# One encoder layer on one core: a weight sum on GpSimd, a copy on ScalarE, swapped chunk pools, longer planned waits and an earlier store

## The chip, the core and the metric

The kernel runs on one core of a Trainium2 chip. The metric is the device time of one execution in microseconds (us). The engines are named as in the profile: PE is TensorE (matmuls; PEld its weight loads), DVE is VectorE, ACT is ScalarE, POOL is GpSimd, SP is SyncE, which issues most DMAs. L90 is line 90 of the kernel.

## The reference

One layer on x of 512 tokens by 1024 channels, all in float32. RMSNorm, then one projection whose columns feed three branches and their sigmoid gates; an output projection with a residual; RMSNorm, SwiGLU with 2816 hidden columns, a residual and a last RMSNorm.

```python
h = rms_norm(x, norm1_g)
u_pool, aq, ak, av, rq, rf, rb, ri, rg, gate_pre = split_cols(h @ w_in)
y_pool = pool_mixer(u_pool, pool_w, pool_scale)
y_attn = diff_attention(aq, ak, av, lam, diff_norm_g, lambda_init)   # 4 heads, two key/query parts each
y_rec = hgrn2_mixer(rq, rf, rb, ri, rg, lb_fwd, lb_bwd, hgrn_norm_g) # 4 heads, scans in both directions
gates = sigmoid(gate_pre)
merged = sum(gates[i] * (y[i] @ w_up[i]) for i in range(3))
x = x + merged @ w_out
gu = rms_norm(x, norm2_g) @ w_ffn_in
x = x + (silu(gu[:, :2816]) * gu[:, 2816:]) @ w_ffn_out
return rms_norm(x, final_norm_g)
```

## The kernel before

**Precision.** Most products are made of three matmuls. Each operand is split into a high part (`whi`, `hT_hi`: a cast on ACT) and a low part (`wlo`, `hT_lo`: the value less its high part, a subtraction on DVE), and hi·hi, hi·lo and lo·hi are summed in PSUM. A weight thus costs a load by SP into a ring of two buffers (`wraw`), a cast on ACT (L185) and a subtraction on DVE (L186) into a ring of three (`wsp`). `Jobs.pump` writes these ahead of the jobs that need them: at most two chunks of the ring that still have unsplit parts, at most three parts held (four in the feed-forward stage). A chunk with a `where` is loaded into a pool of its own as soon as that pool exists and isn't counted among the two. All weight loads are chained in one order on SP.

**Order.** TensorE's instructions keep the order in which the program writes them (`keep_in_program_order` in `mm`, L89, and `transpose`, L97). That order is made by a small planner, `Pipe` (L40 to L74): streams of work (the heads of a mixer and the stream of projection jobs) yield either `("w", us)`, wait so long in planned time, or `("e", event, us)`, wait until so long after an event. The first stream in the list that is free goes next. Planned time is counted from matmul sizes alone; a stall on the chip is unknown to it. The other engines' orders are chosen by a scheduler that simulates the program when it is built; `tc.issue_after(i)`, also through `behind`, keeps what it encloses behind instruction `i` on `i`'s own engine, and does nothing to instructions of another engine.

**PSUM.** `bank("mm")` and `bank("rc")` have three buffers each, `bank("tp")` two.

The places that the change touches, in order of time:

- *Start* (L566 to L597): `norm1_g` is transposed on PE and spread over the partitions in two halves, each copied from PSUM into `g_b` by DVE (L577). `norm_rows` takes a square sum on ACT (L477), rstd on POOL (L148, L142), then multiplies the row by rstd and `g_b` on DVE in two halves (L483). `rows_T` transposes them on PE (L98) into `hT`.
- *Recurrence* (`rec_scan`, L869): after its scan a head waits for the event "V" (the values) and a planned 1.0 us, makes six states (`st`) of `kT` and `v_rec` in two "rc" banks, waits a planned 1.6 us, and makes its outputs in another "rc" bank.
- *Attention* (`att_head`, L1034): a head's first scores wait until 6.0 us after its query and key projections (event `AF{h}`). Scores are two matmuls for each of two parts, with `k` and with `l`, its rest, of which one half is copied by ACT (L1025).
- *First output quarter* (L1253): `quarter_parts` makes two chunks of 256 columns of `w_out`. The first goes to the pool "wx" (made at L1748, when the gate stage's pools have been closed), the second to the ring.
- *Feed-forward*. The 22 column pairs go through a two by two scheme (Strassen-like, seven products for eight) on sums of activation blocks, the "forms" (`Forms.make`: DVE L356, ACT L359), and on sums of weight blocks, which `PairChunk.add` (L259) makes with three DVE additions: 1024 wide (L263) and twice 512 wide (L266, L267) into one buffer, `sums`. A pair has four jobs, `first` to `fourth`; `PairPart.sums_and_split` casts the sums (`shi`, L302) and subtracts (`slo`, L304). Pair 2's sums are written in `third` of pair 1 (L1343), behind the forms' last instructions. `g` (L1350) and `u` (L1355) add PSUM into SBUF, and pair 2's splits stand behind pair 1's `g` on DVE.
- *Tail* (`seven_job`, L1602): four row blocks of the output get their last products, the residual add (L1410), squares (ACT, L1417), the final gain (DVE, L1419), rstd (POOL, L142) and the two halves of `out_store`: ACT scales one and issues its store, DVE the other, SP its store.

Of the kernel before, what the change touches and what calls it, by code (L numbers as in the profile page):

```python
# [33 lines left out]
def strided(t, offset, dims):  # L34

    return bass.AP(tensor=t.tensor, offset=t.offset + offset, ap=[list(t.ap[0])] + [list(d) for d in dims])
# [40 lines left out]
def encoder_kernel(ctx: ExitStack, tc: tile.TileContext, x, norm1_g, w_in, pool_w, pool_scale,  # L77
# [111 lines left out]
    class Jobs:  # L189
# [10 lines left out]
        def add(self, parts, body):  # L200
            self.jobs.append((parts, body))
            for p in parts:
                if p not in self.parts:
                    self.parts.append(p)
                if p.chunk not in self.chunks:
                    self.chunks.append(p.chunk)
# [37 lines left out]
    class PairChunk:  # L244
# [11 lines left out]
                last = nc.sync.dma_start(out=self.raw[:, c], in_=src).ins  # L256
            return last

        def add(self):  # L259
            half = KT // 2 * P  # L260
            sums = self.sums = LAST["ws"].tile([P, 4, half], F32, name="sums", bufs=1)
            w11, w12 = strided(self.raw, 0, [[1, half]]), strided(self.raw, half, [[1, half]])
            nc.vector.tensor_tensor(out=strided(sums, 0, [[2 * half, 2], [1, half]]),  # L263
                                    in0=strided(self.raw, 0, [[3 * half, 2], [1, half]]),
                                    in1=strided(self.raw, 2 * half, [[0, 2], [1, half]]), op=ALU.add)
            nc.vector.tensor_tensor(out=sums[:, 3], in0=sums[:, 2], in1=w11, op=ALU.add)  # L266
            nc.vector.tensor_tensor(out=sums[:, 1], in0=sums[:, 3], in1=w12, op=ALU.add)  # L267

    @contextmanager
    def behind(after):  # L270
# [170 lines left out]
    def quarter_parts(w, c0, n, where=None, skip=0):  # L441

        v = w.rearrange("(kt p) c -> p kt c", p=P)
        for c in range(0, n, 256):
            ch = Chunk(v[:, :, c0 + c:c0 + c + 256], KT, 256, where if c == 0 else None)
            yield slice(c, c + 256), [Part(ch, lambda raw, j=j: raw[:, j:j + 4, :], 4, 256, None, skip)
                                       for j in (0, 4)]

# [124 lines left out]
    for half in range(2):  # L573
        gt = bank("rc", (P, 4, P))
        for j in range(4):
            transpose(gt[:, j, :], g_cols[:, half * 4 + j:half * 4 + j + 1].to_broadcast([P, P]), ident)
        nc.vector.tensor_copy(out=g_b[:, half * 512:half * 512 + 512], in_=gt.rearrange("p a b -> p (a b)"))  # L577

    probe = xg.tile([P, 1024], F32R, name="probe")
    nc.scalar.copy(out=probe, in_=ident.rearrange("p (o c) -> p o c", o=1).to_broadcast([P, 8, P]))  # L580
# [288 lines left out]
    def rec_scan(h):  # L869
# [64 lines left out]
            nc.scalar.copy(out=kT[:, 3 * d:3 * d + 3, :], in_=ps[:, 0:3, :])  # L934
        mark(f"S{h}")
        yield ("e", "V", 0.8)
        yield ("w", 1.0)
        st = rh.tile([P, 6, P], F32, name="st", bufs=2)
        vs = [v_rec[:, b, h * P:(h + 1) * P] for b in range(NB)]
        for d in range(2):  # L940
# [4 lines left out]
            for prev, j in zip((None,) + order, order):  # L945
                own = st[:, 3 * d + j, :]
                if prev is None:
# [2 lines left out]
                total = strided(pyr, toff + d * S + j + d, [[1, 1]])  # L950
                nc.vector.scalar_tensor_tensor(out=own, in0=st[:, 3 * d + prev, :], scalar=total, in1=ps[:, j, :],
                                               op0=ALU.mult, op1=ALU.add)
        yield ("w", 1.6)
        ps = bank("rc")
        for b in range(NB):
            o = ps[:, b * P:(b + 1) * P]
# [77 lines left out]
    def att_head(h):  # L1034
        if h:
            yield ("e", f"QK{h - 1}", 0.0)
        if h > 1:
            yield ("e", f"AN{h - 2}", 0.0)
        yield ("e", f"AF{h}", 6.0)
        t = att.pop(h)  # L1040
        at, (vh, vl), aT, y_attn = ATT["at"], ATT["v"], ATT["aT"], ATT["y"]
        strip = ATT["strip"].tile([P, 896], F32, name="strip")
        nc.sync.dma_start(out=strip, in_=c_dist[h])
        zz = at.tile([P, NB, 2], F32, name="zz")
        rr = at.tile([P, NB], F32, name="rr")
        probs = {}

        def scores(i):
            bs = slice(i * P, (i + 1) * P)
            mx = small.tile([P, 2], F32, name="mx")  # L1050
            ex = []
            for c in range(2):
                ps = bank("rc")
                mm(ps, t[f"q{c}"][:, bs], t[f"k{c}"], True, False)
                mm(ps, t[f"q{c}"][:, bs], t[f"l{c}"], False, True)
                s = at.tile([P, S], F32, name=f"s{c}")

                nc.vector.tensor_tensor_reduce(out=s, in0=strip[:, 384 - P * i:896 - P * i], in1=ps, scale=1.0,  # L1058
                                               scalar=3.0e38, op0=ALU.add, op1=ALU.min, accum_out=mx[:, c:c + 1])
                nc.scalar.activation(out=s, in_=s, func=AF.Exp, scale=-1.0, bias=mx[:, c:c + 1],  # L1060
                                     accum_out=zz[:, i, c:c + 1])
                ex.append(s)

            co = small.tile([P, 2], F32, name="co")
            zn, co = co[:, 0:1], co[:, 1:2]
            nc.gpsimd.tensor_tensor(out=zn, in0=zz[:, i, 0:1], in1=nlam, op=ALU.mult)
            nc.gpsimd.tensor_tensor(out=co, in0=zz[:, i, 1:2], in1=minus1, op=ALU.pow)
            nc.gpsimd.tensor_tensor(out=co, in0=co, in1=zn, op=ALU.mult)
            nc.vector.scalar_tensor_tensor(out=ex[0], in0=ex[1], scalar=co, in1=ex[0], op0=ALU.mult, op1=ALU.add)
            probs[i] = ex[0]  # L1070

        def turn(i):
            bs = slice(i * P, (i + 1) * P)
            p = probs.pop(i)
            pt = bank("tp", (P, NB, P))
            for k in range(NB):
                transpose(pt[:, k, :], p[:, k * P:(k + 1) * P], ident)
            nc.scalar.copy(out=aT[0][:, :, bs], in_=pt)
            nc.vector.tensor_tensor(out=aT[1][:, :, bs], in0=pt, in1=aT[0][:, :, bs].bitcast(F32), op=ALU.subtract)

        scores(0)
        for i in range(NB):
            yield ("w", 1.6 + (0.7 if i == 0 else 0.0))
            if i + 1 < NB:
                scores(i + 1)
            else:
                mark(f"QK{h}")
            yield ("w", 2.4 + (1.0 if i + h == 0 else 0.0))
            if h and i == 0:
                yield ("e", f"PV{h - 1}", 0.0)  # L1090
            turn(i)
        mark(f"T{h}")
        nc.vector.reciprocal(out=rr, in_=zz[:, :, 0])
        yield ("e", "VA", 1.5)
        yield ("w", 1.5)
        ps = bank("rc")
        es = slice(h * P, (h + 1) * P)
        terms = [(vh, aT[0]), (vl, aT[0]), (vh, aT[1])]
        for i, (a, r) in enumerate(terms):
            for k in range(NB):  # L1100
                mm(ps, a[:, k, es], r[:, k, :], i == 0 and k == 0, i == 2 and k == NB - 1)
            yield
        mark(f"PV{h}")
        og, rbp = yield from head_norm(ps, at, gain_a, rr, 1)
        mark(f"AN{h}")
        nc.vector.tensor_tensor(out=og, in0=og, in1=rbp, op=ALU.mult)
        nc.scalar.copy(out=y_attn[0][:, h, :], in_=og)
        nc.vector.tensor_tensor(out=y_attn[1][:, h, :], in0=og, in1=y_attn[0][:, h, :].bitcast(F32),
                                op=ALU.subtract)
# [202 lines left out]
    def ffn_pair_bodies(j):  # L1312
# [30 lines left out]
        def third(part):  # L1343
            f = FF["forms"]
            if j == 1:
                with behind(FF["forms_end"]):
                    pairs[2][1].chunk.add()
            c["sl"] = FF["t"].tile([P, S], F32, name="silu")
            yield from product(c["x"], part, 0, f.d, False)
            on_dve = nc.vector.tensor_tensor(out=c["g"], in0=c["x"], in1=c["g"], op=ALU.add).ins  # L1350
            if j == 1:
                FF["g1"] = (on_dve,)
            nc.scalar.activation(out=c["sl"][:, 256:], in_=c["g"], func=AF.Silu, scale=-1.0)
            yield from product(c["y"], part, 1, f.r22, False)
            nc.vector.tensor_tensor(out=c["u"], in0=c["u"], in1=c["zy"], op=ALU.add)  # L1355
# [56 lines left out]
    def out_sums(b, c0, w, col, out_=None):  # L1412

        x = out_cols(b, c0, w)
        junk = FF["t"].tile([P, S], F32, name="silu")
        col = 4 * b + col
        sq = nc.scalar.activation(out=junk[:, 0:w], in_=x, func=AF.Square, scale=D ** -0.5,  # L1417
                                  accum_out=FF["stats"][:, col:col + 1]).ins
        nc.vector.tensor_tensor(out=x if out_ is None else out_, in0=x, in1=FF["g"][:, c0:c0 + w], op=ALU.mult)  # L1419
        return sq  # L1420
# [181 lines left out]
    def seven_job():  # L1602
# [81 lines left out]
        sv_product(x[1][:, first], 7, 1, False, True, first)  # L1684
        out_add(3, 256, x[1][:, second], ALU.subtract)
        out_add(3, 0, x[1][:, first], ALU.subtract)
        out_sums(3, 0, 256, 1, src[:, first])
        sv_product(own[:, second], 7, 1, True, True, second)
        out_add(3, 256, own[:, second], ALU.subtract)
        sq = out_sums(3, 256, 256, 2, src[:, second])  # L1690
        rstd, on_dve = out_rstd(3, 3)
        with behind((sq, on_dve)):
            out_store(2, late)
        out_store(3, rstd, src)
        yield

    for i, (j, _) in enumerate(PLAIN):
# [137 lines left out]
```

## Time and profile before

| | us |
|---|---|
| median of three runs | 881.21 |
| lowest, highest | 880.99, 881.6 |
| profiled execution, its time | 880.92 |
| its span, first to last instruction | 879.0 |
| PE busy | 866.3 |
| DVE, ACT, POOL busy | 660.8, 448.9, 37.8 |

A timeline row reads: start, time taken, engine, line, operation, output<-input, shape, number of instructions merged into the row, and in brackets the idle time before it with what ended it. A merged row's time runs from its first start to its last end. The profile's waits and busy times are of one execution.

### The profile page before, as it was taken

Reading aid. Unit: us, or ns where it says so; the run is one execution under the profiler, and the core shown is the slowest. Engines: PE = TensorE matmul, PEld = TensorE weight load, DVE = VectorE, ACT = ScalarE, POOL = GpSimd, SP = SyncE. Lnnn points to the kernel's source line nnn. Section 1 sums busy time; section 2 is a strip of 40 time slices with the busy share of each in tenths; the row PEclk is TensorE's granted clock in tenths of the full one; section 3 lists DMA queues with packets and bytes.
Section 4 is the critical chain, followed back from the end, with each engine's and each line's share of the span. In section 5 each row is a group of like instructions: output and inputs, shape, how many; then the busy total and the mean of one; then the engine's idle time right before and its main releaser. Section 6 shows DMA issues by size and latency. Waiting matters only on the chain.

```text
span 879.0 us, 14111 instructions
## 1 busy us (share of the span) xinstructions
PE 866.3 (99%) x5713; PEld 786.4 (89%) x5713; DVE 660.8 (75%) x978; ACT 448.9 (51%) x718; POOL 37.8 (4%) x83
## 2 busy tenths in 40 slices
PE   8999999999999999999999999999999999999996
PEld 7989988888997888899999898999999999988885
DVE  6788655854757787987876645997888888847996
ACT  6544333525747764563355335755655655533563
POOL 2000000000112230000000001000000000000001
PEclk9999999999999999999999999999999999999999
DMA  8330113124133131343331770253433433355002
GB/s 244 97 120 25 50 48 96 48 73 138 45 96 94 52 104 48 97 134 107 96 97 48 263 192 1 54 139 106 135 97 98 137 102 98 120 192 191 1 1 97
DMA packets 115694, 87.54 MB, mean 100 GB/s; under 512 B 3862, under 2 KB 104748, under 8 KB 115628
## 3 DMA queue, kind: packets, MB, share of 16 engines
q1 hardware_dynamic: 115036, 85.57, 32.2%
q8 instruction: 45, 0.74, 0.4%
q10 hardware_dynamic: 592, 1.05, 0.3%
q14 instruction: 21, 0.17, 0.1%
HBM read 84.52 MB, written 2.10 MB: 99 GB/s over the span
## 4 chain that ended last, share of the span: by engine, by line
PE 86%; issue 7%; DVE 3%; DMA 2%; ACT 1%; POOL 1%; POOLq 0%; DVEq 0%; ACTq 0%
PE mm L90 56%; PE rc L90 26%; PE tp L90 2%; PE tp L98 2%; DMA raw<-in_w_out_dram 1%; DVE wlo L186 1%; DVE hrow L483 1%; DMA raw<-in_w_in_dram 0%; ACT whi L185 0%; DVE hT_lo L500 0%; PE rc L98 0%; ACT s L1060 0%; POOL rso L142 0%; DVE g1b L577 0%; ACT l L1025 0%
## 5 line engine op out<-in xcount | busy, mean ns | idle before, releaser
L185 ACT CAST whi<-raw 128x1024 fp32r<-128x1024 f32 (+1 forms) x134 | 127.6, 958 | 141.5 <-PE mm L90 90.7
L186 DVE TENSOR_TENSOR wlo<-raw,whi 128x1024 fp32r<-128x1024 f32 (+1 forms) x134 | 147.5, 1106 | 51.2 <-ACT whi L185 35.4
L90 PE MATMUL mm<-hT_hi,whi 128*128 128x512 f32 (+1 forms) x344 | 82.4, 371 | 0.0
L90 PE MATMUL mm<-hT_hi,wlo 128*128 128x512 f32 (+1 forms) x344 | 81.4, 370 | 0.2 <-DVE wlo L186 0.2
L90 PE MATMUL mm<-hT_lo,whi 128*128 128x512 f32 (+1 forms) x344 | 81.1, 369 | 0.0
L304 DVE TENSOR_TENSOR slo<-sums,shi 128x1024 fp32r<-128x1024 f32 x58 | 70.6, 1218 | 0.3 <-ACT shi L302 0.3
L90 PEld LDWEIGHTS mm<-hT_hi,whi 128*128 128x128 f32 x344 | 59.0, 189 | 9.8 <-ACT hT_hi L496 0.4
L90 PEld LDWEIGHTS mm<-hT_lo,whi 128*128 128x128 f32 x344 | 59.1, 189 | 9.5
L90 PEld LDWEIGHTS mm<-hT_hi,wlo 128*128 128x128 f32 x344 | 58.7, 189 | 9.6 <-DVE wlo L186 0.4
L302 ACT CAST shi<-sums 128x1024 fp32r<-128x1024 f32 x58 | 61.0, 1052 | 4.6 <-DVE sums L266 3.7
L263 DVE TENSOR_TENSOR sums<-raw 128x1024 f32<-128x1024 f32 x29 | 35.4, 1219 | 1.5 <-DMA raw<-in_w_in_dram 1.5
L90 PE MATMUL mm<-y_arena,whi 128*128 128x512 f32 x128 | 32.5, 394 | 0.0
L90 PE MATMUL mm<-whi,y_arena 128*128 128x256 f32 (+1 forms) x192 | 31.9, 316 | 0.2 <-ACT whi L185 0.2
L916 DVE TENSOR_TENSOR kq<-kq,pyr 128x256 f32<-128x256 f32 x48 | 18.2, 421 | 18.1 <-PE rc L90 18.0
L90 PE MATMUL rc<-kq,kc 128*128 128x128 f32 x224 | 31.6, 285 | 0.0
L90 PEld LDWEIGHTS rc<-kq,kc 128*128 128x128 f32 x224 | 30.1, 191 | 1.5
L90 PEld LDWEIGHTS mm<-whi,y_arena 128*128 128x128 f32 x192 | 27.4, 188 | 3.2 <-ACT whi L185 0.8
L885 ACT COPY kc<-kq 128x512 f32<-128x512 f32 x28 | 18.6, 666 | 20.4 <-PE rc L90 12.7
L1060 ACT ACTIVATE s<-s,mx 128x512 f32<-128x512 f32 x32 | 23.1, 721 | 10.9 <-DVE mx L1058 10.7
L90 PEld LDWEIGHTS mm<-y_arena,whi 128*128 128x128 f32 x128 | 23.8, 188 | 5.0
L1350 DVE TENSOR_TENSOR g<-mm,g 128x256 f32<-128x256 f32 x21 | 8.9, 424 | 23.7 <-PE mm L90 23.7
L90 PE MATMUL mm<-fhi,slo 128*128 128x256 f32 x168 | 26.1, 278 | 0.6 <-DVE slo L304 0.5
(386 smaller groups left out, 2045.7 us busy)
## 6 DMA issues: line engine op xcount, KB each, us to landing
raw<-in_w_in_dram SPq DMA_DIRECT2D x44, 512.0 KB, 4.1
raw<-in_w_ffn_in_dram SPq DMA_DIRECT2D x44, 512.0 KB, 5.3
raw<-in_w_in_dram SPq DMA_DIRECT2D x8, 1024.0 KB, 5.2
raw<-in_w_ffn_out_dram SPq DMA_DIRECT2D x7, 1024.0 KB, 4.9
raw<-in_w_out_dram SPq DMA_DIRECT2D x4, 1024.0 KB, 11.1
xin<-in_x_dram SPq DMA_DIRECT2D x4, 512.0 KB, 4.6
raw<-in_w_up_rec_dram SPq DMA_DIRECT2D x2, 1024.0 KB, 6.6
raw<-in_w_up_pool_dram SPq DMA_DIRECT2D x2, 1024.0 KB, 5.1
```

Of the source, the lines that this page charges most:

```text
L90: i = nc.tensor.matmul(out_, lhsT=lhsT, rhs=rhs, start=start, stop=stop, skip_group_check=chain)
L98: tc.keep_in_program_order(nc.tensor.transpose(out_, in_, idn))
L185: nc.scalar.copy(out=hi, in_=view)
L186: LAST["wlo"] = nc.vector.tensor_tensor(out=lo, in0=view, in1=hi.bitcast(F32), op=ALU.subtract).ins
L263: nc.vector.tensor_tensor(out=strided(sums, 0, [[2 * half, 2], [1, half]]), in0=strided(self.raw, 0, [[3 * half, 2], [1, half]]), in1=stri ...
L302: nc.scalar.copy(out=hi, in_=view)
L304: on_dve = nc.vector.tensor_tensor(out=lo, in0=view, in1=hi.bitcast(F32), op=ALU.subtract).ins
L483: on_dve = nc.vector.scalar_tensor_tensor(out=h[:, cs], in0=src[:, cs], scalar=rstd, in1=g_b[:, cs], op0=ALU.mult, op1=ALU.mult).ins
L885: nc.scalar.copy(out=strided(kc, 0, [[2 * n, S // (2 * n)], [n, 2], [1, n]]), in_=strided(kq, 2 * S, [[2 * n, S // (2 * n)], [S + n, 2], [ ...
L916: nc.vector.tensor_tensor(out=xv, in0=xv, in1=tv, op=ALU.mult)
L1060: nc.scalar.activation(out=s, in_=s, func=AF.Exp, scale=-1.0, bias=mx[:, c:c + 1], accum_out=zz[:, i, c:c + 1])
L1350: on_dve = nc.vector.tensor_tensor(out=c["g"], in0=c["x"], in1=c["g"], op=ALU.add).ins
```

## The change

Seven edits:

1. `PairChunk.add` takes an engine, and pair 2's three additions go to POOL. The other pairs' stay on DVE.
2. In `quarter_parts` the second chunk of the first output quarter goes to "wx" and the first to the ring.
3. The second half of `g_b` is copied by ACT.
4. In the recurrence, head 1 waits a planned 4.5 us instead of 1.0 after the values.
5. Heads 0 and 1 wait a planned 2.4 us instead of 1.6 before their outputs.
6. In the attention, heads 2 and 3 wait 7.0 us instead of 6.0 after their projections.
7. Block 2's scaling and store are written after the first half of block 3's sums instead of after its rstd; they stand behind that half's square on ACT, where before they stood behind the second half's square on ACT and rstd's addition on DVE.

```diff
-        def add(self):
+        def add(self, eng=None):
+            eng = eng or nc.vector
...
-            nc.vector.tensor_tensor(out=strided(sums, 0, [[2 * half, 2], [1, half]]),
+            eng.tensor_tensor(out=strided(sums, 0, [[2 * half, 2], [1, half]]),
...
-            nc.vector.tensor_tensor(out=sums[:, 3], in0=sums[:, 2], in1=w11, op=ALU.add)
-            nc.vector.tensor_tensor(out=sums[:, 1], in0=sums[:, 3], in1=w12, op=ALU.add)
+            eng.tensor_tensor(out=sums[:, 3], in0=sums[:, 2], in1=w11, op=ALU.add)
+            eng.tensor_tensor(out=sums[:, 1], in0=sums[:, 3], in1=w12, op=ALU.add)
...
-            ch = Chunk(v[:, :, c0 + c:c0 + c + 256], KT, 256, where if c == 0 else None)
+            ch = Chunk(v[:, :, c0 + c:c0 + c + 256], KT, 256, where if c else None)
...
-        nc.vector.tensor_copy(out=g_b[:, half * 512:half * 512 + 512], in_=gt.rearrange("p a b -> p (a b)"))
+        (nc.scalar.copy if half else nc.vector.tensor_copy)(
+            out=g_b[:, half * 512:half * 512 + 512], in_=gt.rearrange("p a b -> p (a b)"))
...
-        yield ("w", 1.0)
+        yield ("w", 4.5 if h == 1 else 1.0)
...
-        yield ("w", 1.6)
+        yield ("w", 2.4 if h < 2 else 1.6)
...
-        yield ("e", f"AF{h}", 6.0)
+        yield ("e", f"AF{h}", 7.0 if h > 1 else 6.0)
...
                 with behind(FF["forms_end"]):
-                    pairs[2][1].chunk.add()
+                    pairs[2][1].chunk.add(nc.gpsimd)
...
-        out_sums(3, 0, 256, 1, src[:, first])
+        with behind((out_sums(3, 0, 256, 1, src[:, first]),)):
+            out_store(2, late)
...
-        sq = out_sums(3, 256, 256, 2, src[:, second])
-        rstd, on_dve = out_rstd(3, 3)
-        with behind((sq, on_dve)):
-            out_store(2, late)
-        out_store(3, rstd, src)
+        out_sums(3, 256, 256, 2, src[:, second])
+        out_store(3, out_rstd(3, 3)[0], src)
```

More of the change, by code (lines that the diff above doesn't have):

```diff
@@ L262, in add @@
             w11, w12 = strided(self.raw, 0, [[1, half]]), strided(self.raw, half, [[1, half]])
-            nc.vector.tensor_tensor(out=strided(sums, 0, [[2 * half, 2], [1, half]]),
-                                    in0=strided(self.raw, 0, [[3 * half, 2], [1, half]]),
-                                    in1=strided(self.raw, 2 * half, [[0, 2], [1, half]]), op=ALU.add)
-            nc.vector.tensor_tensor(out=sums[:, 3], in0=sums[:, 2], in1=w11, op=ALU.add)
-            nc.vector.tensor_tensor(out=sums[:, 1], in0=sums[:, 3], in1=w12, op=ALU.add)
+            eng.tensor_tensor(out=strided(sums, 0, [[2 * half, 2], [1, half]]),
+                              in0=strided(self.raw, 0, [[3 * half, 2], [1, half]]),
+                              in1=strided(self.raw, 2 * half, [[0, 2], [1, half]]), op=ALU.add)
+            eng.tensor_tensor(out=sums[:, 3], in0=sums[:, 2], in1=w11, op=ALU.add)
+            eng.tensor_tensor(out=sums[:, 1], in0=sums[:, 3], in1=w12, op=ALU.add)
     @contextmanager
```

## The prediction

> **What bounds the kernel now.** I read the page's first part, then what the TensorE (PE) row waits for, then the timeline around each of its gaps.
>
> ```profile
> span 879.0 us, 14111 instructions
> PE 866.3 (99%) x5713; PEld 786.4 (89%) x5713; DVE 660.8 (75%) x978; ACT 448.9 (51%) x718; POOL 37.8 (4%) x83
> ```
>
> TensorE is the bound: 99% of the span, its order written out by a planner. An edit beside it gains only what it takes out of a PE gap, plus what it takes from the stretch behind the last matmul. The profiled execution took 880.92 us, 1.9 more than its span; the three plain runs have a median of 881.21. Sums are made against 880.92; I add 0.29 at the end. Differences under 0.2% (1.8 us) can't be told from none here.
>
> A gap is measured from start to start, since a matmul's end is modelled past the point where the next one can issue: four 128x256 matmuls issue in 0.45, though their row says 0.62 or 0.73. The diff touches six gaps, in order of time.
>
> **Start.** The second half of the gain vector is copied out of PSUM by VectorE (DVE) between the first and second half of the first norm row.
>
> ```profile
> 7.51 1.05 ACT L185 CAST whi<-raw 128x1024 fp32r<-128x1024 f32 x1 [0.57 <-DMA raw<-in_w_in_dram]
> 7.51 0.68 DVE L577 COPY g1b<-rc 128x512 f32<-128x512 f32 x1
> ...
> 8.23 2.08 DVE L483 SCALAR_TENSOR_TENSOR hrow<-xin,rstd,g1b 128x512 f32<-128x512 f32 x3
> ...
> 9.04 0.65 PE L98 MATMUL tp<-ident,hrow 128*128 128x128 f32 x4 [0.73 <-DVE hrow L483]
> ...
> 15.08 2.35 DVE L186 TENSOR_TENSOR wlo<-raw,whi 128x1024 fp32r<-128x1024 f32 x2
> ...
> 16.43 1.05 POOL L148 TENSOR_SCALAR ms<-ss 128x1 f32<-128x1 f32 x1 [2.77 <-ACT hrow L477]
> ...
> 20.22 1.25 PE L98 MATMUL tp<-ident,hrow 128*128 128x128 f32 x8 [0.18 <-DVE hT_lo L500]
> ...
> 39.08 0.58 ACT L895 COPY pt<-rc 128x512 f32<-128x512 f32 x1
> ```
>
> On ScalarE (ACT) the copy costs 0.58 (last row, same shape out of PSUM) and fits the 0.57 in which ACT waits for a weight, from 6.94 (7.51 - 0.57) on. The second half row then starts at 7.6 instead of 8.23: 0.63 for the transposes at 9.04 and all behind them. It must also survive 20.22, where PE waits for work behind the fourth block's norm. That norm's GpSimd (POOL) step at 16.43 took 1.05 because it ended with the DVE pair of 15.08 (17.43), and that pair moves up too. I take 0.55. If the third weight load binds instead, 0; if the simulated schedule puts the copy ahead of ACT's second square, again 0.
>
> **Recurrence.** Heads 0 and 1 make their states back to back.
>
> ```profile
> 115.17 1.50 PE L90 MATMUL rc<-v_rec,kT 128*128 128x128 f32 x12
> ...
> 117.19 0.91 PE L90 MATMUL rc<-v_rec,kT 128*128 128x128 f32 x6 [0.51 <-DVE pt L924]
> ...
> 118.53 0.91 PE L90 MATMUL rc<-v_rec,kT 128*128 128x128 f32 x6 [0.44 <-ACT st L948]
> ...
> 119.19 0.70 PE L90 MATMUL mm<-hT_hi,whi 128*128 128x512 f32 x2
> ```
>
> At 0.11 apiece (118.53 to 119.19 for six), twelve take 1.32 and six 0.66: lost 2.02 - 1.32 = 0.70 and 1.34 - 0.66 = 0.68, together 1.38, waiting for "rc" banks to be emptied. The longer planned wait puts head 1 some 3.5 us later, and projection matmuls that wait for nothing stand in between. The work is the same, only its order changes. The new order has three banks too: a scan level, head 0's output and head 1's two states want four, so one shorter wait may come back. I take 1.2, between 0.6 and 1.38.
>
> **Attention.** Head 2's first scores wait for its second key part.
>
> ```profile
> 277.74 0.40 PE L90 MATMUL rc<-l,q 128*128 128x512 f32 x1
> ...
> 278.51 0.62 ACT L1025 CAST l<-l 64x512 fp32r<-64x512 f32 x1
> ...
> 279.18 0.50 PE L90 MATMUL rc<-l,q 128*128 128x512 f32 x1 [0.81 <-ACT l L1025]
> ...
> 279.52 1.09 PE L90 MATMUL mm<-hT_hi,whi 128*128 128x512 f32 x4
> ```
>
> The wait makes the first matmul after it cost 0.11 more (a row of four 0.73 instead of 0.62), so a 512-wide one takes 0.34 - 0.11 = 0.23 (279.18 to 279.52). From 277.74 stand two, 0.46, and 1.44 passed: 0.98, and 0.11 for the restart, 1.09 lost. One microsecond later the key part (279.13) is there. The planner runs the head's next scores behind the previous head's value product anyway, so the stage's end doesn't move. I take 1.0; if head 3's tail does come later, 0.4 is left.
>
> **First output quarter.** Its first weight chunk sits in a pool whose space comes free only when the gate forms have been read.
>
> ```profile
> 486.51 6.51 SPq L164 DMA_DIRECT2D raw<-in_w_out_dram  x3
> ...
> 496.20 2.00 ACT L185 CAST whi<-raw 128x1024 fp32r<-128x1024 f32 x2 [2.15 <-DMA raw<-in_w_out_dram]
> ...
> 497.30 0.73 PE L90 MATMUL mm<-whi,y_arena 128*128 128x256 f32 x4
> ...
> 500.63 1.54 PE L90 MATMUL mm<-whi,y_arena 128*128 128x256 f32 x12
> ```
>
> Eighteen matmuls stand between the two PE rows, 2.04 at 0.113; 3.33 passed, 1.29 lost. With the pools swapped the first chunk loads into the ordinary ring, ahead of 486.51, and its splits lie before 497. The second chunk takes the late space, issued at about 486.5, there by 496, and is not wanted before 506. SP's queue behind it (the next chunk, the norm gain) moves up or stays. I take 1.2 (0.9 to 1.29).
>
> **Tail.** Block 2's stores move from behind block 3's last sums to between its two halves.
>
> ```profile
> 870.91 0.42 ACT L1417 ACTIVATE silu<-x 128x256 f32<-128x256 f32 x1 [1.55 <-DVE x L1410]
> ...
> 873.12 0.71 ACT L1441 ACTIVATE x<-x,rstd 128x512 f32<-128x512 f32 x1
> ...
> 875.06 0.34 ACTq L1442 DMA_DIRECT2D out_dram<-x  x1
> ```
>
> The same by windows (PE, PEld, DVE, ACT, POOL busy, then clock, DMA share, GB/s), and the page's row of these stores:
>
> ```profile
> 874.00:875.00 1.00, 0.00 (x0) 0.00 (x0) 0.49 (x1) 0.69 (x1) 0.28 (x1) 1.00 0.23 90
> 875.00:876.00 1.00, 0.00 (x0) 0.00 (x0) 0.00 (x0) 0.03 (x1) 0.00 (x0) 1.00 1.01 387
> ...
> out_dram<-x ACTq DMA_DIRECT2D x4, 256.0 KB, 2.6
> ```
>
> The last four stores (1.05 MB) go out together at 387 GB/s, 2.7 us from about 874.8. With block 2's scaling at 871.4 its half is gone by then, and block 3's 0.52 MB takes 1.35 from about 875.8: some 0.5 less. Next late is block 3's own chain (sums, rstd, scaling), not shortened. The added work on ACT (0.71 and an issue) fits before the second square; the other issue goes to SP, which has nothing else queued. I take 0.5 (0.2 to 0.9).
>
> These five sum to 0.55 + 1.2 + 1.0 + 1.2 + 0.5 = 4.45 (ends 2.1 and 5.2).
>
> **The sums on GpSimd.**
>
> ```profile
> 560.90 1.22 DVE L304 TENSOR_TENSOR slo<-sums,shi 128x1024 fp32r<-128x1024 f32 x1
> ...
> 562.04 0.69 DVE L186 TENSOR_TENSOR wlo<-raw,whi 128x512 fp32r<-128x512 f32 x1
> 562.64 1.22 DVE L356 TENSOR_TENSOR flo<-hid,fhi 128x1024 fp32r<-128x1024 f32 x1
> ...
> 563.78 1.22 DVE L263 TENSOR_TENSOR sums<-raw 128x1024 f32<-128x1024 f32 x1
> ...
> 564.74 0.62 PE L90 MATMUL rc<-h_hi,slo 128*128 128x256 f32 x4
> ...
> 564.92 0.42 DVE L1350 TENSOR_TENSOR g<-mm,g 128x256 f32<-128x256 f32 x1
> ...
> 575.11 0.62 PE L90 MATMUL rc<-h_hi,shi 128*128 128x256 f32 x4
> ```
>
> Two POOL rows of the attention, the DVE row beside the first, and the two POOL groups from which a rate can be had:
>
> ```profile
> 238.94 0.55 POOL L1067 TENSOR_TENSOR co<-zz,fixed 128x1 f32<-128x1 f32 x1 [0.52 <-ACT s L1060]
> ...
> 317.73 1.64 POOL L1067 TENSOR_TENSOR co<-zz,fixed 128x1 f32<-128x1 f32 x1 [0.52 <-ACT s L1060]
> 317.74 1.23 DVE L186 TENSOR_TENSOR wlo<-raw,whi 128x1024 fp32r<-128x1024 f32 x1 [0.43 <-ACT s L1060]
> ...
> masks.py:199 POOL TENSOR_SCALAR_AFFINE_SELECT ident<-ident 128x128 f32<-128x128 f32 x1 | 0.3, 292 | 0.1
> ...
> L1820 POOL MEMSET const-float32-1.0<- 128x1 f32 x1 | 0.1, 98 | 0.0
> ```
>
> DVE is rid of 1.22 and two 512-wide adds, as dear as the 512-wide row above (0.69): 2.6. From 564.74 to 575.11 stand 19 rows of four matmuls, 8.61 at 0.113; 10.37 passed, so 1.76 is lost to late DVE results: all that a free move could win. POOL's price for such an add is not shown. The one wide POOL row gives (292 - 98)/128 = 1.5 ns an element with one input; one to two times that is 1.6 to 3.1 us for the first add, half for the others. I take 2.3, 1.2 and 1.2. The Trainium skill's "GPSIMD Engine Reference", section "Performance versus the Vector engine", times a 2048-element add at 4497 ns; the estimate from it is 2.25, 1.1 and 1.1, and no run here shows it yet.
>
> Nothing queues the adds behind the forms: the edge is DVE's and ACT's. They start when the one "sums" buffer is free, 562.1, beside the last forms. There the rows warn: a POOL operation that takes 0.55 alone took 1.64, ending 0.4 after DVE's two-input subtraction did. POOL waits for DVE; whether DVE waits for POOL no row shows, as POOL's are one element wide. I take it to hold both ways, since what POOL waits for can only be something that one of them has at a time. Then: wlo to 562.73, first add to 565.0, flo to 566.25, g to 566.65, and PE's fourth product, due at 565.19, starts at 566.75. Second add to 567.5, wlo 1024 to 568.7, third add to 569.9, wlo 512 to 570.6, u (512 wide too) to 571.2, slo to 572.4. PE wants it at 571.74, after 44 more matmuls from 566.75. Lost: 1.55 + 0.65 and two restarts of 0.11, 2.4 against 1.76: 0.65 worse. If flo gets in first, 0.2 better; if DVE keeps the old order, 0.69 more stands ahead of the first slo and 2.6 (one 1024 and two 512 wide) ahead of the second, worked out alike 2.2 worse. The Trainium skill's "SBUF — State Buffer", section "SBUF: two separate sides", has the port pair that the two engines share held for a whole instruction by whichever starts first, while the other fully blocks; it names DVE's two-input operations against POOL's reads. The rows agree for a waiting POOL. By the rule the part loses, without it it wins up to 1.76.
>
> Sum: 4.45 - 0.65 = 3.8; 880.92 - 3.8 = 877.1, and 877.4 for a median.
>
> **Rivals.** *DVE isn't held up by POOL.* For it: no DVE row beside a POOL one is stretched. The part wins up to 1.7: 881.21 - 6.1 = 875.1. Chance 0.2. *Port held, and DVE in its old order.* The old order has the sums between the two sets of splits, and their going need not move the rest; against it, the schedule is made anew and can take each slo as its sum is there. 881.21 - 4.45 + 2.2 = 879.0, chance 0.12. *The new orders bring new waits*: head 1's states wait for banks again and head 3 ends late, so the 2.2 of those two parts don't come. For it: the rows of 117.19 and 118.53 show that the three banks are what heads wait for, and nothing in a trace of before shows a new order; against it: each changed wait is longer than the gap that it aims at. 881.21 - 1.6 = 879.6, within the 0.2%, chance 0.13. *Slower:* the adds are far dearer. PE's second product of pair 2 needs the second add, a cast and slo; 4.45 is eaten once slo ends at about 576, so the second add after 573.5. That is 1536 elements in 10.8 us, 7 ns an element, near five times the wide row. At 10 ns the part costs 9 us: 885.8. For it: POOL's power takes 0.55 for one element; against it: the 1.5 ns. Chance 0.04. That the edits don't do what they say, 0.01, counts as no change.
>
> **How the numbers follow.** The forecast has 0.5; its own range is 876.2 to 878.6. The range over all cases, 874.7 to 879.8, takes in the first three rivals and leaves out the dear adds and the worst of the rest. Faster: 0.5 + 0.2, most of 0.12 and a little of 0.13 make 0.81. Same 0.14, slower 0.05.
>
> **What would show it.** Right: start-to-start gaps gone near 117, 279 and 498; the stores' last stretch shorter; POOL rows at L263 to L267 of 2.3 and 1.2, and a DVE row near 562 to 569 that starts or ends late beside one. Wrong: those PE gaps back at new places, POOL adds over 5 us, or DVE rows that run through a POOL add unstretched.

## The result and the profile after

| us | before | after |
|---|---|---|
| median of 8 runs each, same chip | 881.40 | 878.47 |
| lowest, highest | 880.76, 882.17 | 878.15, 879.85 |
| profiled execution, its time | 880.92 | 878.23 |
| its span | 879.0 | 876.4 |

The ratio is 0.9972 with a 95% interval of 0.9963 to 0.9981: faster by 2.5 us (1.7 to 3.3). It is estimated from the single executions; the two medians differ by 2.9. 877.4 was forecast; the range held the time, and the gain is about 1 us short of the forecast.

The page's first part, after:

```profile
span 876.4 us, 14114 instructions
PE 865.3 (99%) x5713; PEld 786.2 (90%) x5713; DVE 660.8 (75%) x974; ACT 448.2 (51%) x719; POOL 41.3 (5%) x86
```

TensorE still carries the span, and POOL has 3.5 us more. A kernel whose bound engine is 99% busy in both profiles can only be read from that engine's starts. The same matmul's start, after less before, gives the account; it is called the lag below, and a negative lag means earlier. It reads -0.81 behind the start, -1.77 behind the recurrence (-0.96), -2.59 behind the attention (-0.86, with 0.04 in other places), -3.11 behind the first output quarter (-0.52), -1.87 behind pair 2 (+1.25). From there to TensorE's end nothing moves. The span is 2.57 shorter, so the tail gives 0.70.

**Start.** The timeline after, at the rows that answer to 8.23 and 20.22, with the power that POOL takes between them:

```profile
6.52 2.98 DVE L484 SCALAR_TENSOR_TENSOR hrow<-xin,rstd,g1b 128x512 f32<-128x512 f32 x4 [0.43 <-POOL rstd L142]
7.40 0.56 POOL L142 TENSOR_TENSOR rstd<-ms,mhalf 128x1 f32<-128x1 f32 x1
19.40 1.26 PE L98 MATMUL tp<-ident,hrow 128*128 128x128 f32 x8 [0.18 <-DVE hT_lo L501]
```

DVE runs its four half rows without a break, POOL gets its power in at 7.40, and the place that the gain had to survive (20.22) comes at 19.40.

**Recurrence and attention.** TensorE's timeline after (the states of heads 0 and 1, head 2's output, and a place behind the attention), with the two DVE rows that head 2 waits for:

```profile
114.36 1.50 PE L90 MATMUL rc<-v_rec,kT 128*128 128x128 f32 x12
120.65 1.50 PE L90 MATMUL rc<-v_rec,kT 128*128 128x128 f32 x12
134.51 0.68 DVE L970 TENSOR_TENSOR og<-og,tp 128x512 f32<-128x512 f32 x1
134.82 0.38 PE L90 MATMUL rc<-pt,v_rec 128*128 128x128 f32 x2
135.11 0.34 DVE L953 SCALAR_TENSOR_TENSOR st<-st,pyr,rc 128x128 f32<-128x128 f32 x1
135.50 0.49 PE L90 MATMUL rc<-kq,st 128*128 128x128 f32 x2 [0.31 <-DVE st L953]
...
337.24 0.62 PE L98 MATMUL tp<-ident,rso 128*128 128x128 f32 x4
```

The gaps of 1.38 and 1.09 are gone: head 0's twelve state products start 6.3 us ahead of head 1's, and the scores near 278 run through. But two products that issue in 0.11 each took from 134.82 to 135.50, 0.46 lost, since head 2's last state stands on DVE behind `og` of the head before; the restart costs 0.11 more. And 337.24 starts 0.25 late, behind rstd of the last head, which ends later as its scores were put off.

**First output quarter.** TensorE's timeline after; below it three rows of the same quarter before, since the forecast showed only its first microseconds:

```profile
494.63 1.58 PE L90 MATMUL mm<-whi,y_arena 128*128 128x256 f32 x12
...
503.11 2.05 PE L90 MATMUL mm<-whi,y_arena 128*128 128x256 f32 x16
505.00 1.11 PE L90 MATMUL mm<-wlo,y_arena 128*128 128x256 f32 x8
...
517.25 3.13 PE L90 MATMUL mm<-whi,y_arena 128*128 128x512 f32 x13
```

```profile
506.77 1.98 PE L90 MATMUL mm<-whi,y_arena 128*128 128x256 f32 x16
508.58 1.07 PE L90 MATMUL mm<-wlo,y_arena 128*128 128x256 f32 x8
...
520.37 0.86 PE L90 MATMUL mm<-whi,y_arena 128*128 128x512 f32 x3
```

No wait is left after. Yet sixteen products take 1.89 (503.11 to 505.00) instead of 1.81 (506.77 to 508.58). The whole quarter, 192 products, takes 22.62 after, 0.1178 apiece; before, 497.30 to 520.37 is 23.07, of which 21.75 is 192 times 0.1133 and 1.32 waits. A wait of 1.3 went, and 0.87 of dearer products came. The granted clock is the same (0.999 in the mean after).

**The sums.** The timeline after, DVE, POOL and the two TensorE rows that wait:

```profile
558.92 0.68 DVE L186 TENSOR_TENSOR wlo<-raw,whi 128x512 fp32r<-128x512 f32 x1
559.13 2.72 POOL L264 TENSOR_TENSOR sums<-raw 128x1024 f32<-128x1024 f32 x1 [13.97 <-DVE slo L305]
559.52 3.42 DVE L357 TENSOR_TENSOR flo<-hid,fhi 128x1024 fp32r<-128x1024 f32 x1
561.93 2.15 POOL L267 TENSOR_TENSOR sums<-sums,raw 128x512 f32<-128x512 f32 x1
562.86 0.41 DVE L1352 TENSOR_TENSOR g<-mm,g 128x256 f32<-128x256 f32 x1
563.19 3.67 DVE L186 TENSOR_TENSOR wlo<-raw,whi 128x1024 fp32r<-128x1024 f32 x2
563.32 0.73 PE L90 MATMUL mm<-fhi,whi 128*128 128x256 f32 x4 [1.17 <-DVE g L1352]
564.15 2.16 POOL L268 TENSOR_TENSOR sums<-sums,raw 128x512 f32<-128x512 f32 x1
567.56 0.69 DVE L1363 TENSOR_TENSOR hid<-silu,u 128x512 f32<-128x512 f32 x1
569.45 0.72 PE L90 MATMUL mm<-fhi,slo 128*128 128x256 f32 x4 [0.86 <-DVE slo L305]
```

A row's time holds its wait for the port, so ends are compared with ends. The first add ends at 561.85, 2.25 after the DVE row ahead of it (558.92 + 0.68); `flo`, 1.22 alone, takes 3.42 and ends 1.1 after the add. The second add ends at 564.08, 1.14 after `flo` (562.94); the third (566.31) ends 1.16 after the first of the two merged `wlo`, which ends at 565.15. So they take 2.25, 1.1 and 1.1, and the two engines take turns. `g`, which reads PSUM, runs in its 0.41 in the middle of the second add. TensorE loses 1.33 + 0.11 at 563.32 (due at 561.99 behind four products from 561.54), 1.02 + 0.11 at 569.45, and 0.4 to 0.5 at smaller waits up to 579: 2.9 to 3.0 in all against 1.76 before.

**Tail.** The last transfers after, as two windows (columns as before), and the last power:

```profile
871.62 0.55 POOL L142 TENSOR_TENSOR rstd<-ss,mhalf 128x1 f32<-128x1 f32 x1 [2.71 <-DVE ss L1435]
...
873.00:874.00 1.00, 0.00 (x0) 0.00 (x0) 0.00 (x0) 0.00 (x0) 0.00 (x0) 1.00 0.45 170
874.00:875.00 1.00, 0.00 (x0) 0.00 (x0) 0.00 (x0) 0.00 (x0) 0.00 (x0) 0.80 0.89 354
```

Only block 3's 0.52 MB goes last (170 + 354 KB in two windows), instead of 1.05 MB.

### The profile page after: what moved, and what is told of

The parts are those of the page before. It is cut to its first block, busy times and chain, and to the rows that moved or that the text cites. A ratio compares the mean times of both kernels' runs of the same rounds, so it can differ in the third digit from the quotient of the medians.

```text
span 876.4 us, 14114 instructions
## 1 busy us (share of the span) xinstructions
PE 865.3 (99%) x5713; PEld 786.2 (90%) x5713; DVE 660.8 (75%) x974; ACT 448.2 (51%) x719; POOL 41.3 (5%) x86
## 3 DMA queue, kind: packets, MB, share of 16 engines
q10 hardware_dynamic: 592, 1.05, 0.3%
## 5 line engine op out<-in xcount | busy, mean ns | idle before, releaser
L186 DVE TENSOR_TENSOR wlo<-raw,whi 128x1024 fp32r<-128x1024 f32 (+1 forms) x134 | 149.3, 1118 | 50.9 <-ACT whi L185 32.2
```

The lines of the kernel that those rows point to most:

```text
L186: LAST["wlo"] = nc.vector.tensor_tensor(out=lo, in0=view, in1=hi.bitcast(F32), op=ALU.subtract).ins
```

## The experiments

Each kernel's median, the number of runs, and the ratio to the kernel before on the same chip:

| kernel | us | ratio, 95% interval |
|---|---|---|
| changed kernel | 878.47 (8) | 0.9972, 0.9963 to 0.9981 |
| e1, sums back on DVE | 878.14 (5) | 0.9961, 0.9947 to 0.9975 |
| e2, sums alone | 882.64 (11) | 1.0013, 1.0005 to 1.0022 |
| e3, chunk swap alone | 880.44 (11) | 0.9989, 0.9980 to 0.9998 |
| e4, a transpose ahead of the quarter | 879.25 (7) | 0.9972, 0.9962 to 0.9983 |
| e5, planned waits alone | 879.29 (11) | 0.9976, 0.9967 to 0.9985 |
| e6, start and tail alone | 880.57 (11) | 0.9986, 0.9977 to 0.9994 |
| e7, longer wait in all heads | 880.82 (10) | 0.9986, 0.9977 to 0.9995 |
| e11, best | 877.20 (5) | 0.9953, 0.9940 to 0.9965 |
| e12, two wide products in the quarter | 879.04 (11) | 0.9973, 0.9964 to 0.9982 |

Most of these intervals overlap, so the times alone don't rank the kernels; where a microsecond lies is read from TensorE's starts, in one profile of each kernel. e8, e9 and e10 ran once and are read from their rows alone.

**e1, the sums back on DVE.**

```diff
-                    pairs[2][1].chunk.add(nc.gpsimd)
+                    pairs[2][1].chunk.add()
```

> The changed kernel with pair 2's weight sums given back to VectorE, the other edits kept. Theory (GpSimd and VectorE hold each other up, so the adds cost VectorE their own 2.25 + 1.1 + 1.1 us instead of 2.6): the waits of TensorE between 561 and 575 us sink from 2.9 to about 1.8 us, and the time is about 1.2 below the changed kernel, 877.2, some 4.2 below the kernel before. Rival (the waits come from the new order of VectorE's instructions in the whole schedule, with the activation product ahead of the first weight rest, and not from the adds' place): the waits stay at 2.9 or grow by the 2.6 that VectorE does more, 878.4 or above.

**e2, the sums alone.** The kernel before with edit 1.

> The kernel before with nothing changed but pair 2's sums, on GpSimd. Theory (both engines held up): 1.1 to 1.3 us slower than before, about 882.6; a VectorE row next to the first add takes some 3.4 us instead of 1.22. Rival (VectorE runs on beside GpSimd): up to 1.7 faster, about 879.7. Rival (the loss in the changed kernel belongs to its other edits): no difference from before within 0.3.

In e1's timeline the same stretch reads as it did before the change:

```profile
560.61 1.22 DVE L357 TENSOR_TENSOR flo<-hid,fhi 128x1024 fp32r<-128x1024 f32 x1
572.51 0.74 PE L90 MATMUL mm<-fhi,slo 128*128 128x256 f32 x4 [0.47 <-DVE slo L305]
```

In e2's, `flo` takes 3.42 again:

```profile
563.07 3.42 DVE L357 TENSOR_TENSOR flo<-hid,fhi 128x1024 fp32r<-128x1024 f32 x1
```

From 524 to 604 us of the kernel before, the lag of TensorE's starts grows by 1.25 in e2, by 1.24 in the changed kernel and by 0.00 in e1. e2's time is 1.1 above before (0.4 to 1.9). So the adds on POOL cost 1.25 in both pairs of kernels that differ in nothing else (before and e2, e1 and the changed kernel), as the theory has it. e1's time (878.14, where 877.2 was expected) is too close to the changed kernel's to show it alone: against the changed kernel's, e1's profile lost 0.83 at its start (below) and 0.2 in the attention.

**e3, the swap alone**, and **e4, a transpose between the widths**:

```diff
+            transpose(bank("tp")[:, 0:P], ident, ident) if first else None
             for b in range(3 if first else 0):
```

> The kernel before with nothing changed but the place of the two output weight chunks. Theory (256-wide products that follow a 512-wide run without a wait between issue at 0.118 us apiece until TensorE next waits, and 0.1133 after a wait): the 1.3 of waits near 497 is gone, all 191 products of the quarter are 0.0045 dearer, net 0.4 to 0.5 faster, 880.9. Rival (the 0.118 comes from another edit, or from the run and not the kernel): the quarter issues at 0.1133 and the kernel is 1.3 faster, 880.1.

> The changed kernel with one 128x128 transpose, whose output nobody reads, ahead of the first output quarter. Theory (the dearer rate is a state of TensorE that another kind of work between the two runs breaks, as the transposes near 226 us do): the transpose costs 0.1 to 0.3, the quarter's 191 products issue at 0.1133 and give back 0.86, net 0.55 to 0.75 faster than the changed kernel. Rival (the rate comes from where the operands lie or from the traffic beside): the quarter stays at 0.118 and the kernel is 0.1 to 0.3 slower.

e3's TensorE rows:

```profile
505.67 2.05 PE L90 MATMUL mm<-whi,y_arena 128*128 128x256 f32 x16
507.55 1.11 PE L90 MATMUL mm<-wlo,y_arena 128*128 128x256 f32 x8
```

1.88 for sixteen: the dearer rate belongs to the swap. The lag falls by 0.53 at this place (0.4 to 0.5 expected). e3's profiled execution then lost 0.6 in the feed-forward stage, again at the dearer rate and with no new wait:

```profile
580.20 0.64 PE L90 MATMUL mm<-fhi,shi 128*128 128x256 f32 x4
580.67 0.63 PE L90 MATMUL mm<-flo,shi 128*128 128x256 f32 x4
...
595.13 0.62 PE L90 MATMUL rc<-h_hi,shi 128*128 128x256 f32 x4
595.58 0.62 PE L90 MATMUL rc<-h_lo,shi 128*128 128x256 f32 x4
```

0.47 for four at 580 and 0.45 at 595; 135 products stood at the dearer rate, which the kernel before issued at 0.1133. e3 doesn't edit them, so the same instructions can issue at either rate.

In e4 the transpose cost 0.11 and the quarter stayed at 0.1178 to its end. The theory that another kind of work in between clears the state falls; its rival (0.118 to the end of the quarter) holds.

**e12, two wide products in the quarter.** On e11 (below):

```diff
                 yield from rows_mm(pss[b], m, slice(b * P, (b + 1) * P), parts, 4, range(KT - 2))
+                if b == 0:
+                    junk = bank("tp").rearrange("p (a b) -> p a b", a=2)
+                    for i in range(2):
+                        mm(junk, m[0][:, i, 0:P], parts[0].hi[:, 0:2, :], True, True, True)
```

> The same with two 512-wide products, whose output nobody reads, behind the first block of the first output quarter. Theory (the rate of 0.118 is a state that lasts until the pattern of widths is broken: in one profile two 512-wide products between 256-wide ones ended it): they cost 0.46, the 170 products behind them issue at 0.1133 and give back 0.77, net 0.3 faster than without them. Rival (nothing but a wait ends it, or chance does): 0.118 to the end of the quarter, 0.45 slower.

They cost 0.46, and the products behind them stay at 0.1178. e12's profile has a wait of 1.5 near 568 us that e11's has not, behind a weight's cast that waited 2.26 for its load, so e12's time is not that of the two products alone. The theory falls here too. What stands is a count: in all eight kernels with the swap (after, e1, e3, e4, e7, e8, e11, e12) the quarter issues at 0.1178, in all four without it (before, e2, e5, e6), which wait inside the quarter, its last hundred products, behind the waits, issue at 0.1133.

**e9 and e10, single instructions beside each other.** The first part of e9 lays DVE's and ACT's instructions beside additions on POOL. Its second part, on TensorE: 24 products of 512 and then 64 of 256, with nothing, a transpose, four transposes, or a wait between.

> Nothing of the encoder is computed; single instructions are laid beside each other, so only rows count and not the time. First part, VectorE and GpSimd released together: by the theory that they hold each other up for whole instructions when both read two SBUF tensors, a 128x1024 addition on GpSimd takes 2.2 to 2.3 us alone, four VectorE subtractions (1.22 alone) beside three such additions take 4.9 plus what they wait for GpSimd, some 9 to 11 us in all, and subtractions with one operand in PSUM run on as if alone. By the rival (a shared rate) both would stretch together in every form. Second part, on TensorE, runs of 256-wide products behind runs of 512-wide ones: by the theory that the dearer rate is a state which a direct change of width sets and a wait clears, 0.118 apiece behind 24 wide ones without a wait and behind one transpose, 0.1133 behind a wait; four transposes or two wide products in between are open. By the rival (the rate belongs to the encoder's tiles or traffic) all runs issue at 0.1133.

e9's timeline, first part: what each takes alone, then DVE's subtractions, copies, additions out of PSUM, scalings out of PSUM, and ACT's copies, each beside three additions on POOL:

```profile
14.04 1.23 DVE L80 TENSOR_TENSOR da<-sa,xin 128x1024 f32<-128x1024 f32 x1 [4.28 <-ACT sa L61]
15.30 0.69 DVE L83 COPY da<-sa 128x1024 f32<-128x1024 f32 x1
16.02 0.69 DVE L86 TENSOR_TENSOR da<-sa,ps 128x512 f32<-128x512 f32 x1
...
22.84 11.06 DVE L80 TENSOR_TENSOR dc<-sc,xin 128x1024 f32<-128x1024 f32 x4 [4.23 <-ACT sc L61]
35.16 11.84 DVE L83 COPY dd<-sd 128x1024 f32<-128x1024 f32 x8 [1.26 <-ACT sd L61]
...
47.74 7.19 DVE L86 TENSOR_TENSOR de<-se,ps 128x512 f32<-128x512 f32 x10 [0.74 <-ACT se L60]
48.30 7.21 POOL L92 TENSOR_TENSOR pe<-se,xin 128x1024 f32<-128x1024 f32 x3 [4.76 <-ACT se L61]
```

Four subtractions, 4.9 one after another, take 11.06 beside three additions that take 7.2 where nothing disturbs them: close to the sum of 12.1, and not the longer of the two. Eight copies of 0.69, 5.5 in all, take 11.84: these have one SBUF input and are held up as well. Ten additions with an operand in PSUM take 7.19 for 6.9, and POOL's three take 7.21 beside them. Ten scalings out of PSUM (7.83) and six copies on ACT (6.43) aren't held up either. So DVE and POOL hold each other up, except where DVE takes an operand from PSUM. The Trainium skill's "SBUF — State Buffer", section "Who interferes with whom", has a port pair that is locked for a whole instruction, by two SBUF inputs and by copies in a mode that uses both ports, but not by at most one SBUF input outside such a mode; the rows here agree, though none names the copies' mode.

The second part did not show what the theory said: every run of 256-wide products went at 0.120, behind wide ones, a transpose or a wait alike. In e9 the moving operand (which streams through TensorE) and the stationary one (which is loaded as weights) lay at the same phase, that is, their addresses differ by a multiple of 256 bytes. That gave e10: the moving operand shifted by 0, 32, ... 224 bytes.

> Nothing of the encoder is computed; only the issue rate of 256-wide products counts, by where the moving operand lies against the stationary one (both tiles start at the same phase, the moving one is shifted by 0 to 224 bytes), each shift behind a wait and again behind 24 products of 512. Theory (what the rate can be is set by that shift, as across the encoder's traces products with shift 0 never went below 0.118 and those with 64 had 0.1133 or 0.118 by turns): shift 0 at 0.120 throughout, shift 64 at 0.1133 behind one of the two starts at least, and one of the others at 0.1133 behind both, which would mend the output quarter. Rival (the shift is chance, and the rate a matter of what ran before): all shifts alike.

TensorE's timeline of e10, one row for each shift (the last wide product and 96 of 256), at shifts of 0, 32 and 192:

```profile
38.74 11.91 PE L62 MATMUL b<-mv,st 128*128 128x512 f32 x97
62.35 11.59 PE L62 MATMUL b<-mv,st 128*128 128x512 f32 x97
180.07 11.70 PE L62 MATMUL b<-mv,st 128*128 128x512 f32 x97
```

0.1200, 0.1167 and 0.1178 apiece, start to start (64 is like 192, the others lie between): shift 0 is the dearest, as expected, and the shift does set a rate. But 0.1133 came nowhere, behind a wait or not, so e10 does not reproduce the encoder, where the quarter's products, at a shift of 192 by the programs' addresses, have both rates.

**e5, the planned waits alone** (edits 4, 5, 6), and **e6, start and tail alone** (edits 3, 7).

> The kernel before with nothing changed but the three planned waits of the recurrence and the attention. Theory (what the changed kernel's trace shows there belongs to these waits alone: 1.38 and 1.1 us of gaps gone, 0.57 back where head 2's output waits for its state, 0.25 back ahead of head 3's transposes): 1.6 to 1.8 faster than before, about 879.8. Rival (the two new waits come from the other edits): 2.4 faster, about 879.1. Rival (the longer waits only push work behind): no difference.

> The kernel before with nothing changed but the gain copy at the start and the stores at the end. Theory (the end is worth 0.7; the start is worth little, as with VectorE's rows back to back GpSimd's power behind the third block's norm is held up until they end, and the 0.81 of one profile came from TensorE's quicker first transposes): 0.7 to 0.9 faster, 880.7. Rival (the start is worth its 0.8): 1.5 faster, 880.0.

e5 is 2.1 faster (1.3 to 2.9); its lag falls by 0.91 in the recurrence and 0.85 in the attention, so the two new waits belong to these edits. Its start, in which nothing was edited, is 0.31 earlier than before's. e6 is 1.2 faster (0.5 to 2.0), between theory and rival; its start is 0.36 earlier, its tail 0.7 shorter; 0.6 went in the feed-forward stage as in e3, 134 products at 0.1178 from 574 us on.

That an unedited start moves is told by its first rows. Of e5, and of e1, which has the edit:

```profile
4.73 1.09 PE L98 MATMUL rc<-ident,g1c 128*128 128x128 f32 x8
```

```profile
4.99 1.83 PE L98 MATMUL rc<-ident,g1c 128*128 128x128 f32 x8
7.78 0.94 POOL L142 TENSOR_TENSOR rstd<-ms,mhalf 128x1 f32<-128x1 f32 x1
8.76 1.42 DVE L484 SCALAR_TENSOR_TENSOR hrow<-xin,rstd,g1b 128x512 f32<-128x512 f32 x2 [0.45 <-POOL rstd L142]
```

The first eight transposes took 1.09 in e5 and in the changed kernel, 1.44 in before's profile, 1.83 in e1, 1.91 in e4: TensorE's beginning varies. Start to start, such a transpose takes 0.213 at first and 0.109 later, and the moment of the change lies at 4.6 us of the span in the changed kernel and in e5, at 5.8 before, and at 7.1 in e3, the latest. Against e5 the changed kernel's start is worth 0.50. Where the transposes end later, DVE's pair of half rows is under way when POOL wants to raise the next block's mean to its power; that takes 0.94 instead of 0.56 and ends 0.41 after the pair (8.72 and 8.31 in e1), and the next half row waits for it until 8.76. So it is in e1, whose start at 21 us is 0.02 later than before's, and in e4, e7, e8 and e11, where it is 0.10 to 0.14 earlier. e7's transposes took 1.43, as long as before's, so at an equal beginning the edit won some 0.14 there. In e12 they took 1.04 and 0.67 was won, but it went at 20.30: a weight's cast waited for its load until 15.19 and stood ahead of the fourth block's square on ACT, and the start is 0.09 later. In e6, whose transposes took 1.73, the power began at 7.29, ahead of the pair's second half, and the start is 0.36 earlier.

**e7, the longer wait in all four heads**, against head 2's new wait:

```diff
-        yield ("w", 2.4 if h < 2 else 1.6)
+        yield ("w", 2.4)
```

> The changed kernel with the longer wait ahead of the output in all four heads of the recurrence, not in the first two alone. Theory (head 2's output is planned 0.8 us too early, and projection products can stand there instead): the 0.57 near 135 us is gone, 0.5 faster than the changed kernel, if no other bank is late. Rival (its state is late for another reason, VectorE's queue, and later work takes the wait over): a wait of 0.3 or more shows a few microseconds on, no difference.

TensorE's timeline of e7, at the end of the stage:

```profile
201.06 0.65 PE L98 MATMUL tp<-ident,rso 128*128 128x128 f32 x4 [1.69 <-POOL rso L142]
```

The 0.57 near 135 is gone, four projection products stand in its place. But head 3 ends the stage, and put off it makes TensorE wait 1.8 at 201 (0.46 near 200 in the changed kernel): 0.58 won, 1.3 lost.

**e8, the product `hid` behind the first `slo`.**

```diff
-            nc.vector.tensor_tensor(out=hid_of(j), in0=c["sl"], in1=c["u"], op=ALU.mult)
+            with behind(FF["s12_2"] if j == 1 else ()):
+                nc.vector.tensor_tensor(out=hid_of(j), in0=c["sl"], in1=c["u"], op=ALU.mult)
```

> The changed kernel with pair 1's last activation product (0.69 on VectorE) planned behind pair 2's first weight rest instead of ahead of it. Theory (the term of the sums was mis-sized by this product, which the forecast's order did not have there): the rest starts 0.6 to 0.7 earlier, the second product of pair 2 waits some 0.4 instead of 1.02, and the waits between 561 and 575 us sink from 2.9 to about 2.3; the wait of 1.33 ahead of pair 1's fourth product stays. Rival (the cast of the sum on ScalarE comes last, not VectorE's queue): the 1.02 stays within 0.1.

One run, 879.45 beside 880.68. Pair 2's second product and the next one that needs a rest, on TensorE:

```profile
570.06 0.74 PE L90 MATMUL mm<-fhi,slo 128*128 128x256 f32 x4
573.53 0.74 PE L90 MATMUL mm<-fhi,slo 128*128 128x256 f32 x4 [0.46 <-DVE slo L305]
```

The 1.02 at the second product shrinks to 0.23, and 0.63 comes back at the next one, whose `slo` is now late: 0.2 won, not 0.6. DVE is full in this stretch, so an order only chooses which product waits.

**e11, the best.** e1, and the longer wait in heads 0 to 2.

```diff
+        yield ("w", 2.4 if h < 3 else 1.6)
```

> The changed kernel with pair 2's sums back on VectorE and the longer wait ahead of the output in heads 0 to 2. Theory (the adds cost 1.25 where they were put; head 2's wait near 135 us is a planned time too early, and the 1.3 that the four-head version lost near 200 us came from head 3 alone): the waits between 561 and 575 us at 1.8, none of 0.5 near 135, the 0.46 near 200 as before: 1.2 + 0.5 below the changed kernel, some 4.5 below the kernel before on the same chip. Rival (head 2's later output delays head 3's too, which ends the stage): the gain near 135 is lost near 200, and it is 3.8 below the kernel before.

877.20, 4.1 faster than before (3.1 to 5.3) where 4.5 was expected. The lag falls by 1.50 in the recurrence (0.96 in the changed kernel) and stays level through pair 2. 0.4 went in the attention, where a weight's cast stood ahead of the key part on ACT. In e8 that is plainest: the cast waited 0.86 for its load, and TensorE lost 0.95 in all near 279. The loss differs between kernels that share this stage's edits: 0.4 in e11 and e7, none in the changed kernel and e5.

## Why the prediction was right or wrong

The six parts in the profiled execution, each against the forecast:

| part | forecast | measured |
|---|---|---|
| start | 0.55 | 0.81, of it 0.31 not the edit's |
| recurrence | 1.2 | 0.96 |
| attention | 1.0 | 0.86 |
| first output quarter | 1.2 | 0.52 |
| tail | 0.5 | 0.70 |
| sums on POOL | -0.65 | -1.25 |
| sum | 3.8 | 2.6 |

*Sums.* The mechanism was right and is shown by e2 and e9: the port is held both ways, the adds take 2.25, 1.1 and 1.1. The rival "DVE isn't held up" is out. So is "port held, DVE in its old order" at 2.2: what of the old order came back, `hid` ahead of the first `slo`, added less. The forecast let PE's fourth product start 1.55 late and it started 1.33 late; the mis-sized term is the second one, `slo` at 572.4 against a need at 571.74, for which it reckoned 0.65. Measured is 1.02, and 0.4 more at two places behind it that were not reckoned at all. e8 shows that `hid` alone isn't the cause: with it moved, the lateness goes to the next `slo`. The step that failed is the count of DVE's work for the first `slo` only, where DVE is full up to the next pair.

*First output quarter.* The wait went as forecast, and the step "eighteen matmuls, 2.04 at 0.113" failed for what comes after the wait: all 192 took 0.1178. The forecast took TensorE's rate as fixed by the shape. e3 shows the dearer rate with the swap alone; what sets it isn't settled. It isn't the granted clock, nor the tiles' places, which are the same in the programs before and after; a transpose and two wide products didn't clear it. Only kernels in which TensorE waited inside the quarter had the cheaper rate there. A wait alone doesn't ensure it either, as e3 and e6 issued at 0.1178 right behind the wait at 574; adding a wait to the quarter was not tried.

*Recurrence and attention.* Both gaps went, by the mechanism forecast. The forecast expected one shorter wait back for want of a bank; it came back for want of a state, behind DVE's `og` (e7 and e11 remove it). "The stage's end doesn't move" failed by 0.25 at 337. The third rival was new waits that eat the 2.2 of these two parts; new waits there were, 0.57 and 0.25, and the parts gave 1.82.

*Start.* 0.50 against 0.55 in the one profile where the first transposes are early and no load is late; 0.14 or less in five profiles where they are late, because DVE's rows without a break hold up POOL's power. The forecast looked at that collision at 16.43, and not at the rstd between the rows that it moved. That this part came out near the forecast is luck: the changed kernel's profile had the early transposes. In e12 the forecast's own condition came true, a weight load that binds.

*Tail.* Right in mechanism, 0.70 for 0.5, within its ends.

The errors of the two large misses, 0.68 and 0.6, have the same sign, and the median stands 1.1 above the forecast.

## What to carry to other kernels

In these runs, additions moved from VectorE to GpSimd left VectorE free only where VectorE's own instructions took an operand from PSUM. Where both worked in SBUF, each waited for the other's whole instructions, and GpSimd's took 1.6 to 1.8 times as long (2.25 and 1.1 against 1.22 and 0.69), so the move pays only where VectorE has idle time of that length. When a wait of a bound engine is removed, reckon the stretch behind it again as well: here the engine's own rate changed by 4% for 22 us and took two thirds of the gain. A step put off to fill one gap has to be followed to the end of its stage, since the last head of a stage has nothing behind it that would hide the delay.

## What the runs showed of the hardware

- 256-wide fp32r products issue at 0.1133, 0.1178 or 0.120 us apiece, at granted clocks of 0.997 to 1.0. The relative phase of moving and stationary operand matters (0.1200 at a shift of 0 bytes, 0.1167 at 32, e10), and in the encoder 0.1133 and 0.1178 both occur at one and the same shift, each for a stretch of well over a hundred products. The Trainium skill's "TensorE: Matmul & The Clock Gate", section "Wait — 56ns, not 53.3ns?", has a fixed cost of about 2.5 ns for each matmul of a back-to-back run; one rate for one width, which a reader might take from it, is not what these rows show.
- TensorE's first transposes took 1.04 (e12) to 1.91 us (e3, e4) from one profile to the next, because TensorE issues at half its later rate until a moment that differs: 0.213 apiece and then 0.109, with the change between 4.6 us of the span (the changed kernel) and 7.1 (e3), where its first product starts at 1.34. e10's first 512-wide products show the same: 0.427 apiece for 4.4 us, then 0.230. The granted clock in the windows reads 1.00 before the change as well as after it. The Trainium skill's "TensorE: Matmul & The Clock Gate", section "What you observe", has such a change come about 4 us into sustained matmul activity, give or take 0.5 us; here it came 3.3 to 5.8 us after the first product, a wider range.
